# Long convolutions of an encoder layer: first butterflies by accumulation in PSUM, products in four operations, folded lags of two tiles together

## The chip, the cores and the metric

The kernel runs on one core of a Trainium2 chip. The metric is the device time of one execution in microseconds (us), taken as the median of several runs. Engines: PE (TensorE, matmuls; PEld is its weight loads), DVE (VectorE), ACT (ScalarE), POOL (GpSimd), SP (SyncE, which issues most DMAs).

## The reference, cut to what matters

One encoder layer over a prompt of 1024 and a sample of 256 tokens, each with 16 learned meta tokens in front. A combined input projection feeds attention and a Hyena long convolution of order 2; their outputs are projected, and a squared-ReLU MLP follows. The part that is changed:

```python
def hyena(u, conv_w, filt_fft, hy_bias):
    ...
    z = u[..., HYENA_ORDER * C:].astype(jnp.float32)
    for n in range(HYENA_ORDER):
        y = jnp.fft.irfft(jnp.fft.rfft(z, n=2 * L, axis=1) * filt_fft[None, :, n], n=2 * L, axis=1)[:, :L]
        z = u[..., n * C:(n + 1) * C].astype(jnp.float32) * (y + z * hy_bias[n].astype(jnp.float32))
    return z.astype(u.dtype)
```

## The kernel before

Phase A projects the input and builds the filters' spectra (kept in DRAM as `d_k`); phase B is the attention, with the sample's convolution (`hyena_sample`) woven into its end; phase C runs the prompt's convolution (`hyena`) with the sample's output projection and MLP beside it (`sample_path`, called "side" below), then the prompt's projection and MLP. Weights of the side path are split into two parts for fp32r matmuls (`mm3`, three matmuls for one product, L261 to L263), with half of them split ahead of time into DRAM (`lo_...`).

The prompt's convolution works in four units: order `o` (0, 1) times half of the channels `h` (0, 1), each of 256 channels in two tiles of 128. A unit has two generators. `forward` takes the 1024 positions as eight residues of 128 positions: for each `r` in 0, 2, 1, 3 a `turn` transposes residues r and r+4 on PE (tile `tps`) and ACT copies them to `zt`; `dft` multiplies each with DFT constants (`fc`, fp32, L1452) and adds the meta tokens' part by a second matmul (`mc` times `zm`, fp32r with 96 rows, L1453), into the PSUM tile `dps`. `radix8` then copies residue r+4 out of PSUM with ACT (`bs`), forms sum and difference on DVE (`bpq`), and two further levels of butterflies (`bl`, `bs`), which write the spectrum `xf`. Four times `product` multiplies a quarter of `xf` with the filter's spectrum `kt`, loaded from DRAM: four multiplications (the first on POOL, three on DVE), a subtraction and an addition. `inverse` forms inverse butterflies on DVE (`bv`), transforms back on PE (fp32, `ips`, L1685), multiplies with the gate (`outs`) and adds the lags that wrap around (`folded`, one call for each tile and side: POOL multiplies into `cpr`, DVE reduces into `csum` and adds).

The order of work is written by generators that yield an estimated cost: `weave` always advances the one with the least cost so far, and `beside` lets the side path advance by the cost of the convolution times a rate (`r1`, 0.45). A scheduler then places the instructions on each engine's queue; an engine runs its queue in that order.

```python
gens = [(upto(prev[3]), 1.0)]
if cnt < 4:
    res = []
    gen = forward(cnt // 2, cnt % 2, cnt, res)
    gens.append((upto(gen), 1.0))
yield from weave(*gens)
gens = [(inverse(*prev[:3]), 1.0)]
if cnt < 4:
    gens.append((upto(gen), 1.0))
```

So the products of a unit are woven with the DFT loop of the next, and its inverse with the rest of the next one's butterflies.

Of the kernel before, what the change touches and what calls it, by code (L numbers as in the profile page):

```python
# [13 lines left out]
F32 = mybir.dt.float32  # L14
F32R = mybir.dt.float32r
# [6 lines left out]
P = 128  # L22
# [36 lines left out]
def _dft_constants():  # L59
    n1 = np.arange(128)[:, None]  # L60
    k = np.arange(128)[None, :] + 0.5
    fc = np.zeros((8, 128, 2, 3, 128), np.float32)
    fn = np.zeros((128, 8, 2, 128), np.float32)
    for r in range(8):
        th = 2 * np.pi * k * (8 * n1 + r) / 2048.0
        for i, v in enumerate((np.cos(th), -np.sin(th), np.sin(th))):
            fc[r, :, 0, i], fc[r, :, 1, i] = _split12(v)
        fn[:, r, 0], fn[:, r, 1] = np.cos(th), -np.sin(th)
    mc = np.zeros((96, 10, 2, 128), np.float32)
    for i in range(16):  # L70
        t = i - 16
        for n, res, col in ((2048, t % 8, t % 8), (512, t % 2, 8 + t % 2)):
            th = 2 * np.pi * (np.arange(128) + 0.5) * t / n
            for q, v in enumerate((np.cos(th), -np.sin(th))):
                hi, lo = _split12(v)
                mc[i, col, q], mc[32 + i, col, q], mc[64 + i, col, q] = hi, hi, lo
    kk = np.arange(128)[:, None] + 0.5
    g = np.zeros((128, 4, 2, 2, 272), np.float32)
    c = np.arange(256)
    n = np.concatenate([2 * (c % 128) + c // 128, -1 - np.arange(16)])[None, :]  # L80
    for r in range(4):
        for e in range(2):
            th = 2 * np.pi * (kk + 256 * e) * (4 * n + r) / 2048.0
            for q, v in enumerate((np.cos(th), -np.sin(th))):
                g[:, r, e, q] = v / 1024.0
    return fc, fn, mc, g
# [148 lines left out]
class Builder:  # L235
# [409 lines left out]
    def radix8(self, bank, bp, write, order=(0, 2, 1, 3), kind="f"):  # L645
# [536 lines left out]
    def phase_cf(self):  # L1182
        tc, nc = self.tc, self.nc
        self.sz_stack.close()
        with ExitStack() as left:
            a2, late = [], [[], []]
            wr = self.wr
            with ExitStack() as st:
                pr = self.pool(st, "r_ps", 2, space=PSUM, side="right")
                side = self.sample_path(wr, pr)  # L1190
                with self.keep, ExitStack() as s2:
                    beside(self.hyena(s2), side, (self.dbg.get("r0", 1.0), self.dbg.get("r1", 0.45)))
                a2.append(self.mlp_input(self.pool(left, "f_a0")))
# [229 lines left out]

    def conv_constants(self):
        nc, a = self.nc, self.a
        self.mc = [self.kept.tile([96, 5, 2, P], F32R, name=f"mc{i}", tag=("kh", "kl")[i]) for i in range(2)]
        self.fc = [self.kept.tile([P, 4, 2, P], F32, name=f"fc{i}", tag=("qnh", "qnl")[i]) for i in range(2)]
        self.g0 = self.kept.tile([P, 2, 2, 272], F32, name="g0", tag="vh")
        for i in (1, 0):
            nc.gpsimd.dma_start(self.mc[i], a["c_m"][:, i * 5:i * 5 + 5])  # L1430
            nc.sync.dma_start(self.fc[i], a["c_fn"][:, i * 4:i * 4 + 4])
        nc.sync.dma_start(self.g0, a["c_g"][:, 0])
# [23 lines left out]

    def folded(self, bp, coef, end, front, out, x):
        nc = self.nc
        pr = bp.tile([P, 16, 16], F32, name="cpr", bufs=1)
        s1 = 1 if front else -1  # L1460
        self.tt(pr, mk(end, [[0, 16], [1, 16]]), mk(coef[:, 15:16], [[s1, 16], [-s1, 16]]), ALU.mult, nc.gpsimd)
        cs = bp.tile([P, 16], F32, name="csum", bufs=2)
        nc.vector.tensor_reduce(cs, pr, axis=AX.X, op=ALU.add)
        csv = cs.rearrange("p (n r) -> p n r", n=out.shape[1]) if len(out.shape) == 3 else cs
        self.tt(csv, csv, x, ALU.mult)
        self.tt(out, out, csv, ALU.add)


    def hyena_sample(self, rope, sz, bank):
        nc = self.nc  # L1470
        zms = sz.tile([96, 512], F32R, name="zms")
# [3 lines left out]
        temp = [t[:, i] for t in temp for i in range(2)]  # L1475
# [98 lines left out]
    def hyena(self, st):  # L1574
# [17 lines left out]
        def turn(cols):  # L1592
            pt = pt_.tile([P, 2, 256], F32, name="tps")
            for i, c in enumerate(cols):
                for cc in range(2):
                    nc.tensor.transpose(pt[:, i, cc * 128:cc * 128 + 128], c(cc), self.ident)
            zt = sp.tile([P, 2, 256], F32, name="zt", bufs=2)
            nc.scalar.copy(zt, pt)
            return zt

        dft = lambda *x: self.dft(pd.tile([P, 512], F32, name="dps"), *x)
        folded = lambda *x: self.folded(bp, *x)

        def forward(o, h, cnt, res):
            if o == 0:
# [40 lines left out]
            yield "half"
            for mq in (0, 2, 1, 3):
                t = sp.tile([P, 2, 2, 256], F32, name="kt", bufs=2)
                self.q("lk").dma_start(t, self.d_k[o][h][:, :, mq * 2:mq * 2 + 2])
                run(self.product(xf[:, :, mq * 2:mq * 2 + 2], t, [bp.tile([P, 2, 256], F32, name="bl", bufs=4) for _ in range(4)], self.dbg.get("pc", (0,))))  # L1650
                yield 3.6

        def inverse(o, h, res):
            ends, xf = res
# [7 lines left out]
            for odd in range(2):  # L1662
# [15 lines left out]
                for r, w in ((odd, w0), (odd + 2, w2)):  # L1678
# [13 lines left out]
            for cc in range(2):  # L1692
                ct = 2 * h + cc
                tail = lambda t: mk(t[:, cc, 126:127], [[1, 2], [128, 8]])
                folded(self.cf[:, o, ct, 0], ends[:, cc, 0, 0:1], True, tail(outs), tail(xs))
                if o == 0:
                    folded(self.cb[:, ct, 0], ends[:, cc, 1, 0:1], False, outs[:, cc, C_META:C_S], xs[:, cc, C_META:C_S])
                else:
                    self.q("oh").dma_start(self.d_oh[ct][:, :LP], outs[:, cc, :LP])
# [217 lines left out]
```

## Time and profile before

| | |
|---|---|
| median of 3 runs | 1939.59 us (1938.0 to 1943.59) |
| the profiled execution | 1943.15 us, its span 1941.4 us |
| mean granted clock of TensorE | 0.957 |
| busy share of the span: PE, DVE, ACT, POOL | 91%, 59%, 39%, 36% |
| the prompt's convolution | 687 to 943 us of the span |

The span runs from the first to the last instruction; the time also has what lies around it. A share of busy time is an average over stages with different limits. A matmul's row in the trace is longer than its turn, since matmuls overlap: start-to-start distances tell what one costs in a row of them. An fp32 matmul leaves two records (and two weight loads), an fp32r matmul one.

### The profile page before, as it was taken

To read this page: it belongs to the slowest core of one execution; us is meant where nothing else is said; L and a number is where in the kernel's file an instruction comes from. 1 tells how busy PE (TensorE), PEld (TensorE's weight loads), DVE (VectorE), ACT (ScalarE), POOL (GpSimd) and SP (SyncE) were. 2 spreads that over 40 slices of the span, in tenths; PEclk is the share of its full clock that TensorE was granted. 3 is DMA by queue.
4 is the path that set the end of the run, shared out by engine and by line. 5 is a ranking of instruction groups with operands and counts; after the bars stand their busy time and mean duration, and the time that the engine had idled before them with its cause. 6 is when DMAs were issued, how large, how long until landed. Compare 5 with 4: busy or idle time off the path is not lost.

```text
span 1941.4 us, 26719 instructions
## 1 busy us (share of the span) xinstructions
PE 1775.0 (91%) x9806; PEld 1561.1 (80%) x9806; DVE 1149.4 (59%) x1862; ACT 751.6 (39%) x1362; POOL 689.2 (36%) x660
## 2 busy tenths in 40 slices
PE   7999999887878988998899799899999999999996
PEld 6899999787778777887779678777888888888885
DVE  6588875753446868999642956763333334333347
ACT  6344443443334454332344565544322222222232
POOL 2112113377882210222376743234422222222234
PEclk9899999988999998999899899999999999999997
DMA  4454535367776276767543574345211111111104
GB/s 165 141 177 159 169 111 196 106 202 242 231 246 210 76 255 200 253 222 240 175 139 120 174 233 143 121 130 166 96 45 44 44 44 44 50 52 56 56 5 142
DMA packets 183654, 275.70 MB, mean 142 GB/s; under 512 B 15258, under 2 KB 89952, under 8 KB 183394
## 3 DMA queue, kind: packets, MB, share of 16 engines
q1 hardware_dynamic: 174936, 254.97, 40.3%
q0 software_dynamic: 5872, 17.06, 2.9%
q10 hardware_dynamic: 2714, 1.96, 0.3%
q8 instruction: 77, 1.26, 0.3%
q14 instruction: 55, 0.45, 0.1%
HBM read 210.90 MB, written 60.38 MB: 140 GB/s over the span
## 4 chain that ended last, share of the span: by engine, by line
PE 64%; DVE 15%; DMA 9%; issue 4%; POOL 4%; ACT 4%; SPq 0%; POOLq 0%; ACTq 0%; DVEq 0%
PE p L261 13%; PE p L263 13%; PE p L262 12%; PE pp L261 2%; PE pp L262 2%; PE pp L263 2%; PE ips L1685 2%; PE wps L263 2%; PE wps L261 2%; PE wps L262 2%; DVE bl L275 2%; POOL pre_raw L272 1%; PE dps L1452 1%; DMA w_raw<-in_w_ff 1%; DMA pre_raw<-in_w_ff 1%
## 5 line engine op out<-in xcount | busy, mean ns | idle before, releaser
L272 POOL TENSOR_TENSOR w_lo<-w_raw,w_hi 128x512 fp32r<-128x512 f32 x276 | 383.3, 1400 | 678.7 <-ACT w_hi L269 622.0
L269 ACT CAST w_hi<-w_raw 128x512 fp32r<-128x512 f32 x388 | 237.8, 619 | 441.4 <-PE p L262 293.3
L261 PE MATMUL p<-sh,w_hi 128*128 128x512 f32 (+1 forms) x800 | 284.5, 360 | 11.1 <-DVE acc L275 4.1
L262 PE MATMUL p<-sl,w_hi 128*128 128x512 f32 (+1 forms) x800 | 283.5, 354 | 11.7 <-DVE sl L272 11.6
L261 PE MATMUL p<-a2h,w_hi 128*128 128x512 f32 (+1 forms) x784 | 285.0, 364 | 8.5 <-ACT a2h L282 4.9
L263 PE MATMUL p<-a2h,w_lo 128*128 128x512 f32 (+1 forms) x784 | 282.7, 361 | 8.8 <-DMA w_lo<-lo_w_ff 6.8
L263 PE MATMUL p<-sh,w_lo 128*128 128x512 f32 (+1 forms) x800 | 284.1, 355 | 4.4 <-POOL w_lo L272 4.4
L262 PE MATMUL p<-a2l,w_hi 128*128 128x512 f32 (+1 forms) x784 | 281.1, 359 | 0.1
L275 DVE TENSOR_TENSOR acc<-acc,p 128x512 f32<-128x512 f32 (+1 forms) x284 | 184.8, 656 | 146.4 <-PE p L263 145.9
L261 PEld LDWEIGHTS p<-sh,w_hi 128*128 128x128 f32 x800 | 154.8, 194 | 35.8 <-ACT sh L269 6.2
L262 PEld LDWEIGHTS p<-sl,w_hi 128*128 128x128 f32 x800 | 155.4, 194 | 34.3 <-DVE sl L272 14.2
L263 PEld LDWEIGHTS p<-a2h,w_lo 128*128 128x128 f32 x784 | 153.1, 195 | 32.0 <-DMA w_lo<-lo_w_ff 7.0
L261 PEld LDWEIGHTS p<-a2h,w_hi 128*128 128x128 f32 x784 | 153.5, 196 | 30.7 <-ACT a2h L282 5.9
L263 PEld LDWEIGHTS p<-sh,w_lo 128*128 128x128 f32 x800 | 155.9, 195 | 25.8 <-POOL w_lo L272 5.1
L262 PEld LDWEIGHTS p<-a2l,w_hi 128*128 128x128 f32 x784 | 153.1, 195 | 22.6 <-DVE a2l L278 0.6
L278 DVE SCALAR_TENSOR_TENSOR rl<-p,rs 128x512 f32<-128x512 f32 (+1 forms) x66 | 44.5, 674 | 199.7 <-PE p L263 199.6
L1779 ACT ACTIVATE rl<-rl 128x512 f32<-128x512 f32 (+1 forms) x66 | 40.9, 619 | 235.6 <-DVE rl L278 235.6
L261 PE MATMUL pp<-ah,w_hi 128*128 128x432 f32 x336 | 123.8, 369 | 0.0
L262 PE MATMUL pp<-al,w_hi 128*128 128x432 f32 x336 | 122.6, 365 | 0.0
L263 PE MATMUL pp<-ah,w_lo 128*128 128x432 f32 x336 | 122.3, 364 | 0.0
L269 ACT CAST pth<-sset 128x512 fp32r<-128x512 f32 (+2 forms) x112 | 51.1, 456 | 140.1 <-DVE ptl L272 64.3
L272 POOL TENSOR_TENSOR pre_raw<-pre_raw,pre_hi 128x512 f32<-128x512 f32 x80 | 102.5, 1281 | 5.5
(390 smaller groups left out, 3772.0 us busy)
## 6 DMA issues: line engine op xcount, KB each, us to landing
w_raw<-in_w_ff SPq DMA_DIRECT2D x292, 256.0 KB, 2.8
pre_raw<-in_w_ff SPq DMA_DIRECT2D x64, 256.0 KB, 3.5
lo_w_ff<-pre_raw SPq DMA_DIRECT2D x64, 256.0 KB, 2.7
w_raw<-in_w_o SPq DMA_DIRECT2D x64, 256.0 KB, 3.4
w_lo<-lo_w_ff SPq DMA_DIRECT2D x64, 256.0 KB, 4.1
fct<-in_c_f POOLq DMA_DIRECT2D x32, 384.0 KB, 4.3
w_raw<-in_w_in SPq DMA_DIRECT2D x32, 256.0 KB, 2.9
k<-spec SPq DMA_DIRECT2D x8, 1024.0 KB, 5.1
```

The costliest lines, as they stand in the source:

```text
L261: mm(out, lhsT=ah, rhs=bh, start=start, stop=False)
L262: mm(out, lhsT=ah, rhs=bl, start=False, stop=False)
L263: return mm(out, lhsT=al, rhs=bh, start=False, stop=stop).ins
L269: return self.nc.scalar.copy(out, src).ins
L272: return (eng or self.nc.vector).tensor_tensor(out, src, f(hi), op=ALU.subtract).ins
L275: (eng or self.nc.vector).tensor_tensor(out, a, b, op=op)
L278: (eng or self.nc.vector).scalar_tensor_tensor(out, x, s, y, op0=op0, op1=op1)
L1452: mm(n, lhsT=self.fc[fr // 4][:, fr % 4, i], rhs=zt, start=True, stop=False)
L1685: mm(ps[:, :width], lhsT=w[q][:, ch], rhs=gr[:, e, q, :width], start=i == 0, stop=i == 3)
L1779: nc.scalar.activation(r, r, AF.Square)
```

## The change

Four things change in the convolutions.

1. `radix8_pairs` replaces `radix8` for the prompt. The sum and the difference of residues r and r+4 are accumulated in PSUM: `pair(r, minus)` adds the DFT of residue r, that of r+4 (or of its negated copy `zn`, which ACT writes in `turn`), and the meta tokens' part, whose constants now hold sum and difference. Of residues 2 and 3 ACT copies both results out; those of 0 and 1 stay in PSUM, and DVE goes on with the second level from there.
2. `product` has two multiplications of 1024 columns (the second with the filter's real and imaginary part swapped), a subtraction and an addition, all on DVE, in the prompt and in the sample.
3. `folded2` does the folded lags of both tiles of a unit in one call.
4. The meta constants and `zm` have 128 rows, the added ones zero. The estimated costs and the rate `r1` (0.5) are new.

```diff
-    mc = np.zeros((96, 10, 2, 128), np.float32)
+    mc = np.zeros((128, 10, 2, 128), np.float32)
...
+        for r in (2, 0, 3, 1):
+            for i, b in enumerate(bank(r)):
+                if r > 1:
+                    t[i] = bp.tile([P, 512], F32, name="bs", bufs=2)
+                    nc.scalar.copy(t[i], b)
+                else:
+                    o = t[r, i] = [bp.tile([P, 512], F32, name="bpq", bufs=8) for _ in range(2)]
+                    if i:
+                        pm(v(o[0]), v(o[1]), v(b), rev(t[i]))
+                    else:
+                        pm(o[0], o[1], b, t[i])
+            yield 1.0
+        (e0, e1), (o0, o1), (tp, tm), (u_p, um) = t[0, 0], t[1, 0], t[0, 1], t[1, 1]
...
-                    beside(self.hyena(s2), side, (self.dbg.get("r0", 1.0), self.dbg.get("r1", 0.45)))
+                    beside(self.hyena(s2), side, (self.dbg.get("r0", 1.0), self.dbg.get("r1", 0.5)))
...
+    def folded2(self, bp, coef, cc, end, ce, front, out, x):
+        nc = self.nc
+        pr = bp.tile([P, 2, 16, 16], F32, name="cpr", tag="bl", bufs=2)
+        s1 = 1 if front else -1
+        self.tt(pr, mk(end, [[ce, 2], [0, 16], [1, 16]]), mk(coef[:, 15:16], [[cc, 2], [s1, 16], [-s1, 16]]), ALU.mult, nc.gpsimd)
+        cs = bp.tile([P, 2, 16], F32, name="csum", bufs=2)
+        nc.vector.tensor_reduce(cs, pr, axis=AX.X, op=ALU.add)
...
+            zn = sp.tile([P, 256], F32, name="zn", bufs=1)
+            nc.scalar.activation(zn, pt[:, 1], AF.Copy, scale=-1.0)
+            return zt[:, 0], zt[:, 1], zn
+
+
+        def pair(r, minus, z, m):
+            ps = pd.tile([P, 512], F32, name="dps")
+            mi = 4 * minus + r
+            for i in range(2):
+                n = ps[:, i * 256:i * 256 + 256]
+                mm(n, lhsT=self.fc[0][:, r, i], rhs=z[0], start=True, stop=False)
+                mm(n, lhsT=self.fc[1][:, r, i], rhs=z[1 + minus], start=False, stop=False)
+                mm(n, lhsT=self.mc[mi // 5][:, mi % 5, i], rhs=m, start=False, stop=True)
+            return ps
...
             for _ in range(4):
                 next(rad)
-                yield 1.7
+                yield 2.0
             yield "half"
             for _ in rad:
-                yield 4.5
+                yield 2.6
...
-                run(self.product(xf[:, :, mq * 2:mq * 2 + 2], t, [bp.tile([P, 2, 256], F32, name="bl", bufs=4) for _ in range(4)], self.dbg.get("pc", (0,))))
-                yield 3.6
+                run(self.product(xf[:, :, mq * 2:mq * 2 + 2], t, [bp.tile([P, 2, 2, 256], F32, name="bl", bufs=2) for _ in range(2)]))
+                yield 3.4
...
-    def product(self, x, k, t, pool=()):
-        xr, xi, kr, ki = x[:, 0], x[:, 1], k[:, 0], k[:, 1]
-        tt = lambda i, *x: self.tt(*x, self.nc.gpsimd if i in pool else None)
-        tt(0, t[0], xr, kr, ALU.mult)
-        tt(1, t[1], xi, ki, ALU.mult)
+    def product(self, x, k, t):
+        self.tt(t[0], x, k, ALU.mult)
         yield
-        tt(2, t[2], xr, ki, ALU.mult)
-        tt(3, t[3], xi, kr, ALU.mult)
+        self.tt(t[1], x, k[:, ::-1], ALU.mult)
         yield
-        tt(4, xr, t[0], t[1], ALU.subtract)
-        tt(5, xi, t[2], t[3], ALU.add)
+        self.tt(x[:, 0], t[0][:, 0], t[0][:, 1], ALU.subtract)
+        self.tt(x[:, 1], t[1][:, 0], t[1][:, 1], ALU.add)
```

PE's queue in the DFT loop of the third unit, one residue, before (`tps` is the transpose, `p` a matmul of the side path):

```order
L262 MATMUL p_8654<-a2l,w_hi 128x256
L1452 MATMUL dps<-zt,fc_6345 128x256
L1453 MATMUL dps<-zm,mc_6343 128x256
L1452 MATMUL dps<-zt,fc_6345 128x256
L1453 MATMUL dps<-zm,mc_6343 128x256
L1452 MATMUL dps<-zt,fc_6346 128x256
L1453 MATMUL dps<-zm,mc_6344 128x256
L1452 MATMUL dps<-zt,fc_6346 128x256
L1453 MATMUL dps<-zm,mc_6344 128x256
L1596 MATMUL tps<-ident,outs 128x128 x4
```

The same place of the changed program:

```order
L1661 MATMUL dps<-zt,fc_6345 128x256
L1662 MATMUL dps<-zt,fc_6346 128x256
L1663 MATMUL dps<-zm,mc_6343 128x256
L1661 MATMUL dps<-zt,fc_6345 128x256
L1662 MATMUL dps<-zt,fc_6346 128x256
L1663 MATMUL dps<-zm,mc_6343 128x256
L1661 MATMUL dps<-zt,fc_6345 128x256
L1662 MATMUL dps<-zn,fc_6346 128x256
L1663 MATMUL dps<-zm,mc_6343 128x256
L1661 MATMUL dps<-zt,fc_6345 128x256
L1662 MATMUL dps<-zn,fc_6346 128x256
L1663 MATMUL dps<-zm,mc_6343 128x256
```

Between two transposes stand eight fp32 matmuls with `fc` where there were four, the same four with `mc`, and in both programs six of the side path.

DVE's queue in the same unit's later butterflies, before (`r`, `sl`, `acc` are the side path's, `outs` and `bv` the inverse's):

```order
L275 TENSOR_TENSOR xf<-bl 128x2x256 x2
L278 SCALAR_TENSOR_TENSOR r<-p_8654,rs_7185 128x512
L275 TENSOR_TENSOR xf<-bl 128x2x256 x2
L275 TENSOR_TENSOR outs<-ips,xg 128x4
L275 TENSOR_TENSOR bl<-bpq 128x512
L272 TENSOR_TENSOR sl<-r,sh 128x512
L275 TENSOR_TENSOR bl<-bpq 128x512 x3
L275 TENSOR_TENSOR bv<-bv 128x512
L278 SCALAR_TENSOR_TENSOR r<-p_8777,rs_7185 128x512
L275 TENSOR_TENSOR bs<-bl 128x512 x2
L278 SCALAR_TENSOR_TENSOR xf<-bs,bl 128x2x256 x3
```

And in the changed program:

```order
L276 TENSOR_TENSOR outs<-ips,xg 128x2x128
L276 TENSOR_TENSOR xf<-bpq 128x2x256 x4
L279 SCALAR_TENSOR_TENSOR xf<-bs,bpq 128x2x256 x3
L279 SCALAR_TENSOR_TENSOR r<-p_8735,rs_7177 128x512
L279 SCALAR_TENSOR_TENSOR xf<-bs,bpq 128x2x256
L276 TENSOR_TENSOR outs<-ips,xg 128x4
L276 TENSOR_TENSOR bv<-bv 128x512
L276 TENSOR_TENSOR bl<-xf,kt 128x1024
```

The level from `bpq` to `bl` is gone, and the products, now of 1024 columns, stand right behind the butterflies.

## Rows read from the trace of the kernel before

**Rows 1.** The page, busy time of each engine, share of the span, instructions.
```profile
PE 1775.0 (91%) x9806; PEld 1561.1 (80%) x9806; DVE 1149.4 (59%) x1862; ACT 751.6 (39%) x1362; POOL 689.2 (36%) x660
```

**Rows 2.** Stretch; busy us (count) of PE, PEld, DVE, ACT, POOL; clock; DMA.
```profile
687.00:731.00 44.00, 38.44 (x259) 35.09 (x260) 28.78 (x45) 20.85 (x37) 6.47 (x7) 0.93 0.70 234
731.00:811.00 80.00, 69.67 (x427) 62.95 (x427) 72.77 (x134) 33.66 (x63) 12.20 (x11) 0.91 0.68 218
811.00:864.00 53.00, 49.92 (x329) 45.88 (x328) 51.17 (x97) 17.74 (x32) 9.99 (x10) 1.00 0.70 223
864.00:943.00 79.00, 71.30 (x415) 64.46 (x414) 70.12 (x121) 17.73 (x31) 13.53 (x8) 0.91 0.63 203
687.00:943.00 256.00, 229.33 (x1426) 208.38 (x1427) 222.84 (x394) 89.97 (x161) 42.19 (x36) 0.93 0.67 217
```

**Rows 3.** The chain that ended last, third unit: start us, us, what.
```profile
814.41 0.70 PE dps L1452 x2
...
818.06 0.70 PE dps L1452 x2
...
837.90 1.81 DVE bl L275 x3
```

**Rows 4.** PE in order of time: start us, us, line, operation, records.
```profile
776.68 3.67 PE L1685 MATMUL ips<-g,bv 128*128 128x260 f32 x16
779.99 0.47 PE L261 MATMUL p<-a2h,w_hi 128*128 128x256 f32 x1
780.30 0.28 PE L262 MATMUL p<-a2l,w_hi 128*128 128x256 f32 x1
780.42 0.29 PE L263 MATMUL p<-a2h,w_lo 128*128 128x256 f32 x1
...
815.07 0.60 PE L1452 MATMUL dps<-zt,fc 128*128 128x256 f32 x2
815.32 0.47 PE L1453 MATMUL dps<-zm,mc 96*128 96x256 f32 x1
815.62 0.60 PE L1452 MATMUL dps<-zt,fc 128*128 128x256 f32 x2
```

**Rows 5.** DVE in order of time, third unit.
```profile
816.18 1.88 DVE L275 TENSOR_TENSOR bv<-xf 128x512 f32<-128x512 f32 x3
817.99 1.27 DVE L275 TENSOR_TENSOR bpq<-dps,bs 128x512 f32<-128x512 f32 x2
```

**Rows 6.** ACT by group, 687 to 943: count, busy us, mean ns, idle before.
```profile
L1598 ACT COPY zt<-tps 128x512 f32<-128x512 f32 x16 | 9.4, 587 | 0.7 <-PE tps L1596 0.5
```

**Rows 7.** DVE by group, the same stretch and columns.
```profile
L275 DVE TENSOR_TENSOR bl<-xf,kt 128x512 f32<-128x512 f32 x48 | 38.9, 830 | 1.9 <-DMA kt<-k 1.8
L275 DVE TENSOR_TENSOR xf<-bl 128x512 f32<-128x512 f32 x48 | 33.8, 734 | 0.0
...
L275 DVE TENSOR_TENSOR bpq<-dps,bs 128x512 f32<-128x512 f32 x32 | 20.7, 681 | 14.1 <-ACT bs L653 14.1
...
L278 DVE SCALAR_TENSOR_TENSOR xf<-bs,bl 128x512 f32<-128x512 f32 x16 | 12.2, 819 | 0.0
...
L1463 DVE TENSOR_REDUCE csum<-cpr 128x16 f32<-128x256 f32 x12 | 5.0, 413 | 0.0
L275 DVE TENSOR_TENSOR csum<-csum,xg 128x16 f32<-128x16 f32 x12 | 4.7, 392 | 0.1
...
L272 DVE TENSOR_TENSOR onl<-on,onh 128x1024 fp32r<-128x1024 f32 x1 | 1.2, 1224 | 0.9 <-ACT onh L269 0.9
```

**Rows 8.** POOL by group, the same stretch and columns.
```profile
L275 POOL TENSOR_TENSOR bl<-xf,kt 128x512 f32<-128x512 f32 x16 | 28.9, 1805 | 146.6 <-DVE xf L278 87.4 <-DVE xf L275 49.5 <-DMA kt<-k 9.6
```

**Rows 9.** PE's weight loads by group, the same stretch and columns.
```profile
L1452 PEld LDWEIGHTS dps<-zt,fc 128*128 128x128 f32 x128 | 21.3, 205 | 9.8 <-ACT zt L1598 8.4
...
L1453 PEld LDWEIGHTS dps<-zm,mc 96*128 96x128 f32 x64 | 13.2, 206 | 2.9 <-DVE zm L272 1.0
```

**Rows 10.** Waits of the DMA queue, 690 to 760: total us, times, longest.
```profile
SPq L399 <- PE wps L263: 22.1, 11, 8.0
```

More of the change, by code (lines that the diff above doesn't have):

```diff
@@ L68, in _dft_constants @@
         fn[:, r, 0], fn[:, r, 1] = np.cos(th), -np.sin(th)
-    mc = np.zeros((96, 10, 2, 128), np.float32)
+    mc = np.zeros((128, 10, 2, 128), np.float32)
     for i in range(16):
         t = i - 16
-        for n, res, col in ((2048, t % 8, t % 8), (512, t % 2, 8 + t % 2)):
+        r = t % 8
+        for n, col, sign in ((2048, r % 4, 1), (2048, 4 + r % 4, 1 if r < 4 else -1), (512, 8 + t % 2, 1)):
             th = 2 * np.pi * (np.arange(128) + 0.5) * t / n
-            for q, v in enumerate((np.cos(th), -np.sin(th))):
+            for q, v in enumerate((sign * np.cos(th), -sign * np.sin(th))):
                 hi, lo = _split12(v)
@@ L690, in radix8, with radix8_pairs, pm @@
         write(2)
+    def radix8_pairs(self, bank, bp, write):
+        nc = self.nc
+        v = lambda t: t.rearrange("p (c n) -> p c n", c=2)
+        rev = lambda t: v(t)[:, ::-1, :]
+        t = {}
+        def pm(out_p, out_m, x, y):
+            self.tt(out_p, x, y, ALU.add)
+            self.tt(out_m, x, y, ALU.subtract)
+        for r in (2, 0, 3, 1):
[11 more added lines that the diff above has]
+        (e0, e1), (o0, o1), (tp, tm), (u_p, um) = t[0, 0], t[1, 0], t[0, 1], t[1, 1]
+        out = write(0)
+        pm(out((0, 0), (1, 0)), out((0, 4), (1, 4)), v(e0), v(o0))
+        pm(out((0, 2), (1, 6)), out((0, 6), (1, 2)), v(e1), rev(o1))
+        yield 1.0
+        ca = bp.tile([P, 512], F32, name="bs", bufs=2)
+        cc = bp.tile([P, 512], F32, name="bs", bufs=2)
+        pm(v(ca), v(cc), v(u_p), rev(um))
+        s = math.sqrt(0.5)
+        out = write(1)
+        self.stt(out((0, 1), (1, 7)), v(ca), s, v(tp), ALU.mult, ALU.add)
+        self.stt(out((0, 5), (1, 3)), v(ca), -s, v(tp), ALU.mult, ALU.add)
+        self.stt(out((1, 5), (0, 3)), v(cc), s, rev(tm), ALU.mult, ALU.add)
+        self.stt(out((1, 1), (0, 7)), v(cc), -s, rev(tm), ALU.mult, ALU.add)
+        yield 1.0
+        write(2)
     def filters(self, st, h2):
@@ L1425, in conv_constants @@
         nc, a = self.nc, self.a
-        self.mc = [self.kept.tile([96, 5, 2, P], F32R, name=f"mc{i}", tag=("kh", "kl")[i]) for i in range(2)]
+        self.mc = [self.kept.tile([P, 5, 2, P], F32R, name=f"mc{i}", tag=("kh", "kl")[i]) for i in range(2)]
         self.fc = [self.kept.tile([P, 4, 2, P], F32, name=f"fc{i}", tag=("qnh", "qnl")[i]) for i in range(2)]
@@ L1458, in folded @@
         nc = self.nc
+        s1 = 1 if front else -1
         pr = bp.tile([P, 16, 16], F32, name="cpr", bufs=1)
-        s1 = 1 if front else -1
         self.tt(pr, mk(end, [[0, 16], [1, 16]]), mk(coef[:, 15:16], [[s1, 16], [-s1, 16]]), ALU.mult, nc.gpsimd)
@@ L1466, in folded @@
         self.tt(out, out, csv, ALU.add)
+    def folded2(self, bp, coef, cc, end, ce, front, out, x):
+        nc = self.nc
+        pr = bp.tile([P, 2, 16, 16], F32, name="cpr", tag="bl", bufs=2)
+        s1 = 1 if front else -1
+        self.tt(pr, mk(end, [[ce, 2], [0, 16], [1, 16]]), mk(coef[:, 15:16], [[cc, 2], [s1, 16], [-s1, 16]]), ALU.mult, nc.gpsimd)
+        cs = bp.tile([P, 2, 16], F32, name="csum", bufs=2)
+        nc.vector.tensor_reduce(cs, pr, axis=AX.X, op=ALU.add)
+        csv = cs.rearrange("p c (n r) -> p c n r", n=out.shape[2]) if len(out.shape) == 4 else cs
+        self.tt(csv, csv, x, ALU.mult)
+        self.tt(out, out, csv, ALU.add)
     def hyena_sample(self, rope, sz, bank):
         nc = self.nc
-        zms = sz.tile([96, 512], F32R, name="zms")
+        zms = sz.tile([P, 512], F32R, name="zms")
         self.clear(zms)
@@ L1474, in hyena_sample @@
         temp = [rope.tile([P, 2, 2, 256], F32, name=f"temp{i}", tag=f"qst{1 + i}") for i in range(2)]
-        temp = [t[:, i] for t in temp for i in range(2)]
         zs = sz.tile([P, 4, 272], F32, name="zs", bufs=2)
@@ L1584, in hyena @@
         nc.scalar.dma_start(g3, a["c_g"][:, 1:4, :, :, :260])
-        zm = cp.tile([96, 512], F32R, name="zm")
+        zm = cp.tile([P, 512], F32R, name="zm")
         self.clear(zm)
@@ L1598, in turn @@
             nc.scalar.copy(zt, pt)
-            return zt
-        dft = lambda *x: self.dft(pd.tile([P, 512], F32, name="dps"), *x)
-        folded = lambda *x: self.folded(bp, *x)
+            zn = sp.tile([P, 256], F32, name="zn", bufs=1)
[10 more added lines that the diff above has]
+            return ps
         def forward(o, h, cnt, res):
@@ L1622, in bank @@
             def bank(r):
-                if r < 4:
-                    cur["zt"] = turn([lambda cc, x=x: zs[:, cc, x * 128:x * 128 + 128] for x in (r, r + 4)])
-                return dft(cur["zt"][:, r // 4], r, r, m)
+                z = turn([lambda cc, x=x: zs[:, cc, x * 128:x * 128 + 128] for x in (r, r + 4)])
+                for minus in range(2):
+                    yield pair(r, minus, z, m)
             def write(part):
@@ L1635, in write @@
                 return out
-            rad = self.radix8(bank, bp, write, kind="c")
+            rad = self.radix8_pairs(bank, bp, write)
             for _ in range(4):
                 next(rad)
-                yield 1.7
+                yield 2.0
             yield "half"
             for _ in rad:
-                yield 4.5
+                yield 2.6
             xf = cur["xf"]
@@ L1691, in inverse @@
                     yield 3.2
[L1692 to L1699, printed above, removed]
+            tail = lambda t: mk(t[:, 0, 126:127], [[C_S, 2], [1, 2], [128, 8]])
+            self.folded2(bp, self.cf[:, o, 2 * h, 0], 62, ends[:, 0, 0, 0:1], 32, True, tail(outs), tail(xs))
+            if o == 0:
+                self.folded2(bp, self.cb[:, 2 * h, 0], 62, ends[:, 0, 1, 0:1], 32, False, outs[:, :, C_META:C_S], xs[:, :, C_META:C_S])
+            else:
+                for cc in range(2):
+                    self.q("oh").dma_start(self.d_oh[2 * h + cc][:, :LP], outs[:, cc, :LP])
             z1[h] = outs
```

## The prediction

> **What bounds the kernel now.** The page gives TensorE 91% busy [rows 1], but that is a share over the whole program, and a matmul's row lasts longer than its turn on the engine. So I looked for the stage that the diff touches: the long convolutions of the prompt, 687 to 943 us, cut into four units at the first DFT matmul of each. Per stretch [rows 2] the busy VectorE (DVE) stands at 73 of 80, 51 of 53 and 70 of 79 us in units 2 to 4, and only 29 of 44 in the first. ACT and POOL are far from full. The chain of work [rows 3] alternates: PE through the DFT loop (steps 3.65 us apart: 814.41, 818.06), then DVE through butterflies, products and inverse butterflies.
>
> PE's own load I take from turns, not from busy time. Eight fp32 matmuls of 256 to 260 columns are 16 records; from their start to the second side matmul behind them are 780.30 - 776.68 = 3.62 us, less one side matmul 3.50, so **0.438 us each** [rows 4]. A side matmul (fp32r) takes 0.12 (same group: 780.30 to 780.42). In the DFT loop a pair of one fp32 and one fp32r "meta" matmul takes 0.55 to 0.56 (815.07 to 815.62), which is 0.438 + 0.12 again. With these turns, and 0.11 for a transpose (estimated from the 0.12), the matmuls that stand in PE's order between the first DFTs of the units come to:
>
> unit 1: 16 DFT x 0.438 + 16 meta x 0.12 + 18 transposes + 192 side x 0.12 = 33.9 of 44 us; unit 2 (32 inverse matmuls, 290 side): 60.4 of 80; unit 3 (199 side): 48.8 of 53; unit 4 to the last inverse matmul (64 inverse, 224 side): 65.1 of 79. Together 208 of 256 us. **The loss, 48 us, is all that a lighter DVE can give back**: 10, 20, 4 and 14 us by unit. Some is not DVE's: the granted clock is 0.91 to 0.93 in units 1, 2 and 4 [rows 2].
>
> **The change part by part.**
>
> *Butterflies in PSUM.* The sums and differences of residues r and r+4 are now accumulated by PE: a pair has two fp32 matmuls for each half, where it had one. That is 4 more per residue, 16 per unit, 64 in all: 64 x 0.438 = **+28 us of PE**, at full clock. The loop step of unit 3 was 3.65 us; by the order it now holds 8 x 0.438 + 4 x 0.12 + 4 transposes + 6 side = 5.1. It has no cover of its own there: PE is what the chain runs through. DVE had 26 operations of 512 columns per unit (8 + 8 + 4 + 2 + 4) and has 18: 32 fewer at 0.60 (three in a row take 816.18 to 817.99 [rows 5]) = **-19 us of DVE**.
>
> *A negated copy on ACT.* 16 copies of 256 columns, each at most the 0.59 of the 512-column one [rows 6]: under 9 us on an engine with 90 of 256 us busy. Only the minus half waits for it, and two matmul groups of the plus half stand ahead. I take 0; if the cover went, up to those 9 us.
>
> *Products.* Three multiplications on DVE plus one on POOL become two of 1024 columns, all on DVE. The one 1024-column row undisturbed is 1.22 us, its turn some 1.14 (the row of 512 is 0.68 with a turn of 0.60) [rows 5, 7]: 2 x 1.14 + 2 x 0.60 = 3.48 against 5 x 0.60 = 3.0, 16 times: **+8 us of DVE**. But POOL's 16 (1.8 us each [rows 8]) go, and with them a disturbance: DVE's products average 0.83, its sums 0.73, its scaled butterflies 0.82, where the same size undisturbed takes 0.68 [rows 7]. 48 x 0.15 + 48 x 0.05 + 16 x 0.14 = **-12 us**. The lower bound is 0, since POOL's folded lags stay and may disturb as much. The Trainium skill (SBUF — State Buffer, "Who interferes with whom") has the shared port pair as an exclusive lock: a DVE operation with two SBUF inputs and a POOL operation that reads SBUF exclude each other for a whole instruction. By that rule each of the 16 POOL operations could hold one DVE operation for up to its own 1.8 us, 29 us rather than 12, and the second rival would gain up to 17 us more. The trace agrees in kind, and its sum is 12.
>
> *Folded lags of two tiles together.* 18 fewer small DVE operations: six reductions of 0.41 merge into larger ones (about -0.15 each pair), twelve of at most 0.39 fall away [rows 7]: between -1 and -6, I take **-4**.
>
> *Meta constants filled to 128.* The matmul's weight load takes 0.206 us with 96 rows and 0.205 with 128 [rows 9], and the 0.55 pair leaves it the plain 0.12. I take **0**.
>
> *Weave costs.* By the order the side matmuls up to the last inverse one are 708 where they were 705: they only move between the units (251, 215 and 242 for 290, 199 and 224). So nothing is handed to the stage behind. The sample's convolution in the attention stage loses 8 DVE operations, 0 to -5 us beside the softmax; I take 0.
>
> **The sum.** PE +28, DVE -27 (-19 + 8 - 12 - 4). PE's load by unit becomes 40.9, 62.7, 57.7 and 74.2, together 235.5 us. Now each unit ends by what is last. Unit 1 waited for weight loads whose buffers PE frees (22 us on the DMA queue [rows 10]) and DVE waited 14 us for ACT copies that follow PE [rows 7]; DVE is not its bound, so its waits stay nearly all: 41 + 8 = 49 us (was 44). Unit 2 is the one with DVE full and PE slack, and gets fewer side matmuls: DVE 73 - 7, PE 63; I take 75 (was 80). Unit 3 had 4 us of loss: PE must now issue 57.7, DVE falls to some 44; 60 (was 53). Unit 4: the DFT loop +7, the DVE chain behind it -7, the last inverse transform, alone on PE, unchanged; 80 (was 79). Sum 264 for 256: **+8 us**. The profiled execution took 1943.15 us (span 1941.4), so 1951; the median of the runs shown is 1939.59, 3.6 below it, so **1948** for a median.
>
> **The rivals.**
>
> *No change (27%).* The PE's loss shrinks to 20 us, 8% of the stage, which is what unit 3 shows now (4.2 of 53). 235.5 + 20 = 256, a median near 1940. For it: the side matmuls can fill any gap that the static order leaves. Against: unit 1's waits have nothing to do with DVE.
>
> *Faster (18%): DVE is what makes PE wait, everywhere.* Then taking 27 us from a DVE that is 89 to 97% full in units 2 to 4 [rows 2] lets PE run nearly without gaps: a loss of 5% gives 248 us, -8, a median of 1932. It decides once the loss is under 14 us. Against: no unit before has a loss so small, and unit 1 alone had 10.
>
> *The added matmuls are not hidden, and DVE's relief gives nothing (10%).* The loss stays 48: 283 us, +27, 1967. Its mechanism: the two buffers "bl" now serve products and POOL's lags, so a product can queue behind a reduction that waits for POOL, and PE's inverse matmuls behind the product. It decides if that happens in every unit; the order sets POOL's lags early in a unit, which speaks against it.
>
> *The fill does something (under 3%, inside the second rival).* Read by starts, the matmul after a meta matmul starts 0.30 us later (815.32 to 815.62 [rows 4]), 0.18 more than 0.12; if those 96 rows cost it, 64 x 0.18 = 12 us come back: 252, 1936. Against: a full side matmul behind fp32 matmuls shows the same 0.31 (779.99 to 780.30 [rows 4]).
>
> **Numbers.** The likeliest case, slower by 4 to 14 us, has 45%; the 10% above is slower too. So slower by over 0.3% (5.8 us, about what a measurement of this kernel can tell) 0.55, within 0.3% 0.27, faster 0.18. Range 1932 to 1961: from the faster rival's time to the middle between the likeliest and the unhidden case. The likeliest one's own range is 1944 to 1954.
>
> **What would show it.** Right: DFT loop steps of some 5.2 us in units 2 to 4; unit 3 near 60 us; DVE busy down by about 27 us over the stage, its sums near 0.68 us each rather than 0.73; meta matmuls with the same turn. Wrong: a unit 3 at or under 54 us, or a first unit no longer than 44, would mean that PE's added matmuls found cover that I don't see; and a change behind the last inverse matmul would mean that the weave's numbers matter more than the matmuls.

## The result and the profile after

The changed kernel takes 1956.91 us (median of 4 runs, 1952.85 to 1957.95), the kernel before 1940.5 (4 runs). Over all runs side by side the ratio is **1.0070, 95% interval 1.0044 to 1.0096**: 13.6 us slower, with bounds of 8.5 and 18.6. The profiled execution took 1957.14 us (span 1955.4), 14.0 above that of before.

The page of the changed kernel, busy time of each engine:

```profile
PE 1796.4 (92%) x9934; PEld 1582.1 (81%) x9934; DVE 1122.9 (57%) x1788; ACT 758.4 (39%) x1378; POOL 666.0 (34%) x638
```

Against [rows 1] DVE is 26.5 us lighter and PE 21.4 heavier. The same stretches as in [rows 2], from the first DFT matmul of a unit to that of the next, and to the last inverse matmul:

```profile
689.50:742.45 52.95, 46.95 (x290) 42.71 (x290) 24.61 (x37) 21.90 (x41) 0.57 (x3) 0.90 0.58 196
742.45:813.78 71.33, 66.37 (x419) 60.94 (x420) 60.74 (x112) 31.77 (x62) 6.94 (x5) 0.98 0.68 216
813.78:872.34 58.56, 58.54 (x378) 54.16 (x378) 46.58 (x80) 20.38 (x39) 4.47 (x5) 1.00 0.70 219
872.34:955.80 83.46, 77.30 (x462) 71.13 (x462) 64.79 (x103) 20.60 (x37) 5.52 (x2) 0.96 0.65 206
689.50:955.80 266.30, 249.17 (x1547) 228.93 (x1548) 196.73 (x329) 94.64 (x176) 17.51 (x15) 0.96 0.66 210
```

The units went from 44, 80, 53 and 79 us to 53, 71, 59 and 83; the stage from 256 to 266. DVE fills 61 of 71 us in unit 2 where it had 73 of 80, and in unit 3 PE is busy in 58.54 of 58.56 us. Of the 14 us, 10.7 lie in the stage, 2.4 ahead of it and 0.9 behind.

The chain that ended last, unit 3 (start us, us, what):

```profile
813.82 0.67 PE dps L1661 x2
...
819.14 0.70 PE dps L1661 x2
...
824.49 0.67 PE dps L1661 x2
...
834.96 0.43 PE dps L1662 x2
839.11 1.10 PE ips L1747 x5
```

A step of the DFT loop is now 5.32 to 5.35 us (813.82, 819.14, 824.49), where [rows 3] had 3.65, and the chain does not leave PE's rows up to the inverse transform. Inside a step, PE in order of time:

```profile
816.28 0.59 PE L1662 MATMUL dps<-zn,fc 128*128 128x256 f32 x2
816.53 0.47 PE L1663 MATMUL dps<-zm,mc 128*128 128x256 f32 x1
816.84 0.59 PE L1661 MATMUL dps<-zt,fc 128*128 128x256 f32 x2
817.26 0.59 PE L1662 MATMUL dps<-zn,fc 128*128 128x256 f32 x2
```

From 816.84 to 817.26 an fp32 matmul has its turn, 0.43 us (0.42 by these rounded starts, 0.43 in the chain's rows above). From 816.28 to 817.26 two of them and one meta matmul take 0.98: that leaves 0.12 for the meta matmul with 128 rows, as with 96 [rows 4]. Nothing waits in front of the matmuls that read the negated copy (`zn`).

DVE by group over the stage (columns as in [rows 7]):

```profile
L276 DVE TENSOR_TENSOR bl<-xf,kt 128x1024 f32<-128x1024 f32 x32 | 38.7, 1222 | 2.9 <-DMA kt<-k 2.9
L276 DVE TENSOR_TENSOR bv<-xf 128x512 f32<-128x512 f32 x32 | 24.5, 782 | 4.9 <-PE ips L1747 4.9
...
L276 DVE TENSOR_TENSOR xf<-bl 128x512 f32<-128x512 f32 x32 | 20.9, 688 | 0.1
L276 DVE TENSOR_TENSOR bpq<-dps,bs 128x512 f32<-128x512 f32 x32 | 20.7, 684 | 23.4 <-PE dps L1663 23.4
...
L279 DVE SCALAR_TENSOR_TENSOR xf<-bs,bpq 128x512 f32<-128x512 f32 x16 | 10.1, 688 | 0.0
```

The sums that stood at 734 ns and the scaled butterflies at 819 are at 688, the wide products at 1222. The idle time ahead of the butterflies (`bpq`) grew from 14.1 to 23.4 us, and ends with PE's DFT where it ended with ACT's copy. Before, all of it lay in unit 1; now 18 us lie there and 5 in units 3 and 4.

### The profile page after: what moved, and what is told of

The parts are those of the page before. It is cut to its first block, busy times and chain, and to the rows that moved or that the text cites. A ratio compares the mean times of both kernels' runs of the same rounds, so it can differ in the third digit from the quotient of the medians.

```text
span 1955.4 us, 26865 instructions
## 1 busy us (share of the span) xinstructions
PE 1796.4 (92%) x9934; PEld 1582.1 (81%) x9934; DVE 1122.9 (57%) x1788; ACT 758.4 (39%) x1378; POOL 666.0 (34%) x638
## 4 chain that ended last, share of the span: by engine, by line
PE 69%; DVE 11%; DMA 9%; POOL 4%; issue 3%; ACT 3%; SPq 1%; POOLq 0%; ACTq 0%; DVEq 0%
PE p L262 14%; PE p L264 14%; PE p L263 13%; PE ips L1747 3%; PE pp L263 2%; PE pp L264 2%; PE pp L262 2%; POOL pre_raw L273 2%; PE wps L264 2%; PE wps L263 2%; PE wps L262 2%; DMA pre_raw<-in_w_ff 1%; PE dps L1661 1%; PE dps L1662 1%; PE dps L262 1%
## 5 line engine op out<-in xcount | busy, mean ns | idle before, releaser
L263 PE MATMUL p<-a2l,w_hi 128*128 128x512 f32 (+1 forms) x784 | 276.7, 353 | 0.7 <-DVE a2l L279 0.7
```

The costliest lines, as they stand in the source:

```text
L263: mm(out, lhsT=ah, rhs=bl, start=False, stop=False)
```

## The experiments

Each was timed beside the kernel before on the same chip, and the ratio is to that kernel; one per cent is 19.4 us. A difference of two ratios is uncertain by 4 to 7 us. Each trace is one execution, and executions of one kernel lie up to 15 us apart (those of e9 from 1931.48 to 1946.85 us; the traces of e2, e6 and e10 are of the shortest of their executions, those of e4 and e9 of the longest), so a stage that differs by a few us proves nothing by itself. From each trace, in us: where the stage begins, its four units, its length, the side matmuls (`wps`, `p`) that stand in it, and what lies behind its last inverse matmul.

| kernel | begins | units 1 to 4 | stage | side | behind |
|---|---|---|---|---|---|
| before | 687.1 | 43.7, 80.0, 53.4, 78.5 | 255.6 | 905 | 998.7 |
| changed | 689.5 | 53.0, 71.3, 58.6, 83.5 | 266.3 | 900 | 999.5 |
| e1 one matmul | 689.0 | 47.4, 69.5, 51.6, 75.3 | 243.9 | 900 | 999.0 |
| e2 no pairs | 684.6 | 45.4, 73.7, 52.1, 80.7 | 251.8 | 947 | 993.5 |
| e3 old rates | 687.8 | 51.6, 72.5, 57.3, 82.4 | 263.8 | 879 | 1002.6 |
| e4 fill | 690.8 | 47.3, 78.4, 53.3, 78.5 | 257.6 | 905 | 997.9 |
| e5 pairs | 688.9 | 53.3, 75.3, 58.8, 86.9 | 274.3 | 876 | 1002.8 |
| e6 products | 686.7 | 45.4, 74.5, 50.2, 81.9 | 252.0 | 962 | 988.9 |
| e7 folded lags | 690.3 | 45.9, 75.7, 53.6, 83.2 | 258.3 | 903 | 999.1 |
| e8 no negation | 689.7 | 53.2, 71.4, 58.6, 82.6 | 265.8 | 900 | 1000.2 |
| e9 product on DVE | 692.5 | 44.9, 74.7, 54.6, 87.9 | 262.1 | 980 | 990.5 |
| e10 changed, own buffer | 685.6 | 51.9, 71.0, 58.6, 83.4 | 264.9 | 900 | 999.2 |
| e11 folded, own buffer | 690.3 | 43.1, 75.5, 53.1, 79.2 | 250.9 | 890 | 1000.1 |
| e12 changed, folded apart | 689.0 | 52.7, 75.5, 58.3, 80.3 | 266.8 | 900 | 1001.6 |

**e1, the matmuls' price.** The second of the two accumulated matmuls is left out of the changed kernel:

```
  mm(n, lhsT=self.fc[0][:, r, i], rhs=z[0], start=True, stop=False)
- mm(n, lhsT=self.fc[1][:, r, i], rhs=z[1 + minus], start=False, stop=False)
  mm(n, lhsT=self.mc[mi // 5][:, mi % 5, i], rhs=m, start=False, stop=True)
```

> The changed kernel without the second accumulated matmul of each pair (64 fp32 matmuls of 256 columns left out, so the sum and the difference are not formed; VectorE, ScalarE and the order of the rest stay). Theory (the 64 added fp32 matmuls at 0.438 us are what the time is paid for, and VectorE's relief is real): nearly all of their 28 us comes off, 1927 to 1934 us, about 0.995 of the kernel before, with the four units together some 240 us. Rival 1 (the slowdown comes from the weave's numbers or from shared buffers, the matmuls lie in gaps): 1950 to 1957 us. Rival 2 (half hidden, VectorE or the weights are last again as soon as TensorE is relieved): about 1943 us.

Measured: 1933.41 us, ratio 0.9951 (0.9934 to 0.9967). From 1.0070 that is 23 us, uncertain by 6, and 22.4 by the stage (266.3 to 243.9). The windows of its units and of the stage:

```profile
689.00:736.40 47.40, 41.50 (x259) 37.85 (x259) 24.42 (x37) 22.16 (x41) 0.65 (x3) 0.85 0.65 222
736.40:805.90 69.50, 62.87 (x388) 56.82 (x388) 61.43 (x112) 31.57 (x62) 4.80 (x5) 0.93 0.69 218
805.90:857.50 51.60, 51.58 (x346) 48.08 (x345) 44.27 (x80) 20.38 (x39) 4.07 (x5) 1.00 0.79 253
857.50:932.80 75.30, 70.05 (x430) 64.50 (x430) 64.60 (x103) 20.70 (x37) 5.14 (x2) 0.95 0.72 228
689.00:932.80 243.80, 226.00 (x1419) 207.25 (x1420) 194.73 (x329) 94.81 (x176) 14.66 (x15) 0.93 0.71 229
```

DVE has the same load as in the changed kernel (194.7 and 196.7 us), so this kernel also shows what DVE's relief is worth with PE as before: 9.5 us under the kernel before (6 to 13), 11.7 by the stage. Some of the 64 matmuls' 28 us may be made good by the granted clock, whose means over the units (shares of 2.4 GHz) are 0.85, 0.93, 1.00 and 0.95 here and 0.90, 0.98, 1.00 and 0.96 with them. They did not fill gaps: PE is idle for 243.80 - 226.00 = 17.8 us of the stage here and for 266.30 - 249.17 = 17.1 with them.

**e2, everything but the pairs.** In the changed kernel `radix8`, `dft`, `bank` and the weave's numbers are those of before; the level-two tiles are halves of the products' wide tiles:

```
- rad = self.radix8_pairs(bank, bp, write)
+ rad = self.radix8_c(bank, bp, write, kind="c")
```

> The changed kernel with the first butterflies back on VectorE and with the old weave costs; products in four operations, folded lags together and the fill stay. Theory (by the terms of the sum: TensorE as before, VectorE 4 us lighter by the products without GpSimd's disturbance and 4 by the folded lags, and about half of what VectorE saves is returned as time): 1934 to 1939 us, 2 to 6 under the kernel before. Rival 1 (the products on VectorE alone are heavier in the stages where it is full, GpSimd's share had been worth more than its disturbance): 1944 to 1950 us. Rival 2 (half of the slowdown is not the pairs): 1947 to 1950.

Measured: ratio 0.9982 (0.9963 to 1.0001), 3.5 us under the kernel before. The theory's size; whether it is faster at all is just inside the uncertainty. So in the company of the other edits the pairs cost 17 us, uncertain by 6, where their matmuls alone cost 23.

**e3, the weave's numbers.**

```
  next(rad)
- yield 2.0
+ yield 1.7
...
  for _ in rad:
- yield 2.6
+ yield 4.5
...
- yield 3.4
+ yield 3.6
...
- self.dbg.get("r1", 0.5)
+ self.dbg.get("r1", 0.45)
```

> The changed kernel with only the weave's numbers as before (1.7, 4.5, 3.6 and 0.45). Theory (the numbers only shift side matmuls from one unit to another, as all are placed by the last inverse matmul in any case): 1953 to 1961 us, same as the changed kernel, with units of other lengths. Rival (the new numbers are what costs): at or under 1948 us.

Measured: ratio 1.0065 (1.0044 to 1.0086), as the changed kernel: 1 us less, uncertain by 6. The numbers are no part of the loss that can be measured.

**e4, the fill alone, on the kernel before.**

```
- mc = np.zeros((96, 10, 2, 128), np.float32)
+ mc = np.zeros((128, 10, 2, 128), np.float32)
```

(and `self.mc`, `zm`, `zms` of 128 rows.)

> The kernel before with nothing but the meta constants and the meta rows filled from 96 to 128 partitions. Theory (a matmul and a weight load take the same with 96 and 128 rows): same as before, 1938 to 1943 us, and the first DFT matmul of the prompt's convolutions at 687 us as before, so the 2.4 us by which the changed kernel's profile comes late to that point are not the larger constants. Rival 1 (the larger constants, 160 KB more each on GpSimd's DMA queue, delay the sample's convolution): that point at 689 to 690, time 2 to 3 us longer. Rival 2 (the 96 rows had cost a reload): about 12 us shorter.

Measured: ratio 0.9990 (0.9975 to 1.0004), the same. Its stage begins at 690.8, but the theory's 687 was no mark: over the fourteen traces of the table the beginning lies between 684.6 and 692.5 with or without the fill. The changed kernel's 2.4 us ahead of the stage are inside that scatter, and nothing ties them to the change.

**e5, the pairs alone, on the kernel before** (`radix8_pairs`, `pair` and `zn` as in the diff above; the lags' GpSimd product takes its space in the products' four buffers).

> The kernel before with the pairs alone (first butterflies accumulated in PSUM, negated copy; products, folded lags, fill and weave's numbers as before, the lags' buffer taken from the products' four as the space demands). Theory (64 matmuls cost the 23 us that leaving them out gave back, and the 19 us less of VectorE return about 6): 1956 to 1961 us, ratio about 1.0085, slower than the whole change. Rival (the products, lags and the rest of the change bring nothing, all of it is the pairs): 1.0065. Rival 2 (VectorE's relief by the butterflies is worth more than that, the rest of the change costs): at or under 1.004.

Measured: 1967.9 us, ratio 1.0126 (1.0105 to 1.0148), 24 us slower and more than any of the three had. DVE's 19 us of butterflies return nothing that can be seen: 24, uncertain by 4, is the price of the matmuls (23 in e1, 28 by their turns). But the shared buffers may have a part in it (e11).

**e6, the products alone, on the kernel before** (`product` as in the diff above).

> The kernel before with the products alone in four operations, all on VectorE. Theory (by its terms 8 us more of VectorE's own work, 12 less by GpSimd's disturbance gone, and less than half of the net returned): ratio 0.998 to 1.000. Rival 1 (all of the gain without the pairs comes from here): 0.997. Rival 2 (the product moved from GpSimd is heavier than the disturbance): 1.001 to 1.004.

Measured: 1935.04 us, ratio 0.9957 (0.9943 to 0.9971), 8 us faster (6 to 11); rival 1, and beyond it. Of the versions that leave nothing out it is the fastest by its median ratio, under both kernels; only e2's interval overlaps with its own. Its DVE groups over the stage:

```profile
L275 DVE TENSOR_TENSOR bl<-xf,kt 128x1024 f32<-128x1024 f32 x32 | 38.6, 1218 | 2.2 <-DMA kt<-k 2.2
L275 DVE TENSOR_TENSOR xf<-bl 128x512 f32<-128x512 f32 x48 | 31.1, 682 | 0.1
...
L278 DVE SCALAR_TENSOR_TENSOR xf<-bs,bl 128x512 f32<-128x512 f32 x16 | 10.1, 681 | 0.0
```

Against [rows 7] (38.9, 33.8 and 12.2) DVE is 5 us lighter, as the terms +8 and -12 said (-4), and all of it comes back as time; whether more than all, the interval leaves open.

**e7, the folded lags alone, on the kernel before** (`folded2` as in the diff above; the product's four tiles are halves of two).

> The kernel before with the folded lags of two tiles together alone. Theory (4 us less of VectorE, spread over the ends of four units): ratio 0.998 to 1.0. Rival (the larger GpSimd multiplication comes late or disturbs VectorE for longer): 1.001 to 1.003.

Measured: ratio 1.0032 (1.0016 to 1.0047), 6 us slower: the rival or a little more, and the theory fell.

**e8, no wait for the negated copy.**

```
- mm(n, lhsT=self.fc[1][:, r, i], rhs=z[1 + minus], start=False, stop=False)
+ mm(n, lhsT=self.fc[1][:, r, i], rhs=z[1], start=False, stop=False)
```

> The changed kernel in which the difference's second matmul reads the plain transposed rows and not their negated copy (so sums stand where differences should; all matmuls stay, only nothing waits for the copy). Theory (the copy is hidden behind the two matmul groups of the sum): as the changed kernel, ratio 1.006 to 1.008. Rival (TensorE waits for it in the DFT loops, 16 times up to 0.59 us): 1.002 to 1.004.

Measured: ratio 1.0065 (1.0042 to 1.0089). The copy is hidden.

**e9, the product's GpSimd operation moved to VectorE, on the kernel before.**

```
- self.dbg.get("pc", (0,))
+ self.dbg.get("pc", ())
```

> The kernel before with nothing but its one GpSimd multiplication per product moved to VectorE: six operations of 512 columns, no wide ones. Theory (what the products gave back, ratio 0.9957, came from taking GpSimd's 1.8 us multiplication out of the chain and off VectorE's back, not from the width of the new operations): 0.994 to 0.998. Rival (the gain is in two operations of 1024 columns where there were four, and VectorE is 9.6 us heavier here): 0.999 to 1.003.

Measured: ratio 1.0000 (0.9982 to 1.0018): the rival. Its DVE groups over the stage:

```profile
L275 DVE TENSOR_TENSOR bl<-xf,kt 128x512 f32<-128x512 f32 x64 | 41.9, 684 | 6.2 <-DMA kt<-k 6.2
L275 DVE TENSOR_TENSOR xf<-bl 128x512 f32<-128x512 f32 x48 | 30.9, 683 | 0.0
...
L278 DVE SCALAR_TENSOR_TENSOR xf<-bs,bl 128x512 f32<-128x512 f32 x16 | 10.0, 681 | 0.0
```

The disturbance is gone: 830, 734 and 819 ns [rows 7] became 684, 683 and 681. That is 48 x 0.146 + 48 x 0.051 + 16 x 0.138 = 11.7 us, the prediction's 12, and sixteen more operations take it up again. Only with the wide form (38.6 us for what takes 41.9 here) is the products' edit a gain.

**e10, the changed kernel with another buffer for the lags.**

```
- pr = bp.tile([P, 2, 16, 16], F32, name="cpr", tag="bl", bufs=2)
+ pr = bp.tile([P, 2, 16, 16], F32, name="cpr", tag="bpq", bufs=8)
```

> The changed kernel with the folded lags' products written to the eight butterfly buffers instead of one of the two that the products use. Theory (GpSimd's lags and the products queue on the same two buffers, which is what makes the folded lags cost 5 to 6 us rather than give 4): ratio 1.003 to 1.005. Rival (the folded lags cost by themselves, by GpSimd's longer multiplication beside VectorE, or their cost is not in this kernel): 1.006 to 1.008.

Measured: ratio 1.0082 (1.0059 to 1.0106): the rival; the 5 to 6 us that the theory gave to the sharing are not there in the changed kernel. Yet its trace differs, in these groups of POOL and DVE over the stage:

```profile
L276 DVE TENSOR_TENSOR bv<-xf 128x512 f32<-128x512 f32 x32 | 21.4, 686 | 3.5 <-PE ips L1747 3.4
...
L276 POOL TENSOR_TENSOR cpr<-ends,cf 128x512 f32<-128x512 f32 x4 | 5.1, 1279 | 141.7 <-DVE bs L276 141.7
```

The inverse butterflies (`bv`) fell from 782 to 686 ns, 3 us in all, and the time did not move by an amount that can be measured (2 us more, uncertain by 7). In the kernel before they stood at 683, so the 782 came with the change:

```profile
L275 DVE TENSOR_TENSOR bv<-xf 128x512 f32<-128x512 f32 x32 | 20.8, 683 | 3.0 <-PE ips L1685 2.9
```

**e11, the folded lags alone with that buffer** (e7 with e10's line).

> The kernel before with the folded lags of two tiles together alone, their GpSimd product in the eight butterfly buffers and not in the products'. Theory (the sharing was the cost): 0.998 to 1.000. Rival (the folded lags cost by themselves): 1.002 to 1.004.

Measured: ratio 1.0015 (1.0000 to 1.0031), between the two. Beside the old products, with a GpSimd operation in the same buffers, the sharing may be half of e7's loss (3 us, uncertain by 4); the intervals overlap, and it stays open. The pairs alone (e5) share buffers in the same way.

**e12, the changed kernel with the lags again tile by tile** (`folded` for each `cc`, as before, in that buffer).

> The changed kernel with the folded lags again tile by tile (pairs, products, fill and weave's numbers stay; the lags' GpSimd product in the butterfly buffers). Theory now (the folded lags of two tiles together cost some 5 us also beside the pairs, so that without them the pairs' 23 us less the products' 8 and a little more remain): ratio 1.003 to 1.005. Rival 1 (they matter in neither direction here): 1.006 to 1.008. Rival 2 (they save the 4 us of VectorE as the prediction had it, or the parts add up as they were measured alone, 24.5 - 8.4 us): 1.008 to 1.010.

Measured: ratio 1.0086 (1.0062 to 1.0110), not the theory; the ratio is in rival 2's range, and the interval holds rival 1's too. Without the folded lags the changed kernel takes 3 us more, uncertain by 7: they may save the 4 us of the prediction or nothing, but here they don't cost 5.

## Why the prediction was right, and where its size was off

Slower was right, and the reason too: PE pays for what DVE is spared. The forecast was +8 us; the ratio says 13.6 (8.5 to 18.6), the trace 10.7 in the stage. The median that was named, 1948, and the likeliest case's own range to 1954 lie below the measured 1956.9.

**PE +28, costed without cover: nearly right.** e1 takes 23 us off (17 to 29). The turn (0.43 us), the loop step (5.3 for a forecast 5.2) and unit 3 (58.6 for 60) came as said. Whether the 5 us between 23 and 28 are real, the ratios don't settle.

**DVE -27: right in busy time** (222.8 to 196.7 us), and so are most of its parts: sums and scaled butterflies at 0.69, the disturbance of 12 (e9). Two were off and partly cancel: the lags' rows on DVE (`csum`, and `outs` with `csum`) fell by 7 us, 13.7 to 6.3, where 4 was taken, and the inverse butterflies rose by 3, which no term had.

**What DVE's relief returns is the step that was off.** The sum let PE's loss fall from 48 to 28.5 us, a return of 20. By the trace it fell to 266.3 - 235.5 = 31, and e1 takes this apart: relief alone returns 9.5 to 12. The other 5 or 6 us are added matmuls that cost less than their full-clock turns. By the traces they did not fit into gaps: PE's idle time is 17.8 us without and 17.1 with them, while the mean granted clock over the stage is 0.93 and 0.96. That points to the clock, but it is one execution of each kernel. Nor did a us of DVE return the same everywhere, though the sum by units took it so. The products' 5 us returned 8 (e6); the butterflies' 19 returned nothing that can be seen alone (e5) and some 6 in company (23 - 17, each uncertain by 6). For the lags' 4 (e12) and the inverse butterflies' 3 (e10) nothing and a full return both lie inside an uncertainty of 7. The butterflies are fed by the DFT loop, which the same edit lengthens: DVE's idle time ahead of `bpq` grew by 9.3 us, 4 in unit 1 and 5 in units 3 and 4. That this is why they return so little is argued, not shown. Whether the parts measured alone (24.4 - 8.3 + 6.2 - 1.9 = 20 us, uncertain by 6 to 7) come to less together (13.6), the runs don't settle either; the shared buffers, which may cost 3 us each in e5 and e7, could be counted there twice.

**By units.** Unit 1 was given +5 and got 9: its loss was lowered from 10 to 8 us with no reason, when DVE is not its bound. In the traces with the second matmul (changed, e3, e5, e8, e10, e12) it is 51.6 to 53.3, in the others 43.1 to 47.4, so its own +7 of matmuls or a little more, and the profile of before had a short one. Unit 4 was given +1 and got 5: -7 for the DVE chain was too much. In e1, whose matmuls are those of before, it is only 3.2 shorter than before, with 18 side matmuls (2.2 us) more in it: some 5 of the 7. The forecast of unit 4 did not name those 2.2 us, though its load of 74.2 has them. One of its waits is no work of DVE's, as the chain of the changed kernel shows:

```profile
922.64 0.60 DVE xf L276
923.39 0.33 SPq L1760
923.77 0.43 SPq L1760
924.25 1.10 SPq L1719
925.39 1.23 SPq L1719
926.68 0.36 issue
927.04 7.12 DMA w_lo<-lo_w_ff
934.20 0.58 PE p L264
```

A weight load stands behind the stores and loads of the convolution on SP's queue, and PE waits for it. This wait is not a cost of the change. PE's waits for that load in unit 4, before and changed (total us, times, longest):

```profile
PE p L263 <- DMA w_lo<-lo_w_ff: 6.8, 1, 6.8
PE p L264 <- DMA w_lo<-lo_w_ff: 6.1, 1, 6.1
```

It stands in unit 4 of all fourteen traces, with 4.6 to 8.4 us; no edit took it away. Unit 2, with fewer side matmuls, gave 8.7 where 5 was taken.

**The costs set at nothing** held: the negated copy (e8), the fill (e4), the weave's numbers (e3). In the count of side matmuls the prediction's 705 for before is 713 by its own numbers for the units (290, 199 and 224); with 708 after it, five (0.6 us) go to the stage behind, as 905 and 900 in the table say.

**The rivals.** No change is excluded by the interval, just. Faster needed a loss under 14 us; it stayed at 31. The unhidden case's mechanism, GpSimd's lags in the products' buffers, does not show in the changed kernel (e10); but a price of +24 with no return is what the pairs cost by themselves (e5), where those buffers are shared too, so that there the mechanism is not excluded. The rule of the Trainium skill on VectorE and GpSimd (SBUF — State Buffer, "Who interferes with whom") has the two exclude each other for a whole instruction. The 29 us that the prediction drew from it is too much: it takes the GpSimd rows at 1.8 us, which hold GpSimd's own waiting. At the 1.2 us of a GpSimd multiplication of that size with nothing beside it (e10, shown in the last section) the bound is 19, and e9 frees 11.7.

## What to carry to other kernels

A microsecond taken from an engine need not come back as a microsecond of time (here 26 us less of VectorE returned some 10): ask for each removed operation who is waiting just there, not how full the engine is over the unit. Moving additions into fp32 accumulation costs a full matmul turn each (0.43 us for 256 columns here, and two of them for each VectorE addition of 512 columns that is spared, whose own turn is 0.60), and where the loop that feeds VectorE is PE's own, part of the relief can turn into longer waiting (9 us here). Split a change of several edits before keeping it: here one of four edits, the wide products, was worth 8 us, and the pairs took 17 to 24.

## What the runs showed of the hardware

GpSimd and VectorE hold each other up, and either can be the one that waits. POOL and DVE of the changed kernel in order of time, unit 2:

```profile
771.45 4.02 POOL L276 TENSOR_TENSOR cpr<-ends,cf 128x512 f32<-128x512 f32 x1 [78.03 <-DVE xf L276]
```

```profile
771.81 0.69 DVE L276 TENSOR_TENSOR bv<-xf 128x512 f32<-128x512 f32 x1
...
774.29 0.69 DVE L279 SCALAR_TENSOR_TENSOR r<-p,rs 128x512 f32<-128x512 f32 x1
774.89 1.13 DVE L276 TENSOR_TENSOR bv<-bv 128x512 f32<-128x512 f32 x1
```

The same in unit 3, and last the multiplication in e10 with nothing beside it on DVE:

```profile
818.53 1.58 POOL L276 TENSOR_TENSOR cpr<-ends,cf 128x512 f32<-128x512 f32 x1 [7.67 <-DVE xf L276]
820.07 1.65 POOL L276 TENSOR_TENSOR cpr<-ends,cb 128x512 f32<-128x512 f32 x1
818.97 3.90 DVE L276 TENSOR_TENSOR bv<-xf 128x512 f32<-128x512 f32 x3
833.02 1.21 POOL L276 TENSOR_TENSOR cpr<-ends,cf 128x512 f32<-128x512 f32 x1 [27.37 <-DVE bs L276]
```

The multiplication takes 1.21 us undisturbed. In unit 2 it took 4.02, while the VectorE operations beside it kept their 0.69 back to back and only the last took 1.13: there GpSimd waited. In unit 3 VectorE pays: three inverse butterflies took 3.90 us, where the kernel before had 1.88 [rows 5], 1.0 us more for each of the two multiplications. Of the six multiplications of the changed kernel three held up a VectorE operation for 1.0 us, two for 0.4 and one for nothing. The Trainium skill's page named above lets the two exclude each other for a whole instruction. The trace agrees: a VectorE operation that is held loses up to 1.0 us to a multiplication of 1.2.

What lies behind the stage followed the count of side matmuls inside it: at 0.12 us for each, the two together are 1104 to 1110 us in all fourteen traces. So e6's 252.0 us stage, only 3.6 shorter than before, also took 57 more side matmuls in, and 9.8 us fell off behind it: a stage's length alone does not tell what an edit in it is worth.
